# First stage of a hybrid attention block: the hand-written order of weight splits, column sums and products

## The chip, the core and the metric

The kernel runs on one core of a Trainium2 chip. The metric is the device time of one execution in microseconds (us). The engines are TensorE (PE in the profile, its weight loads PEld), VectorE (DVE), ScalarE (ACT), GpSimd (POOL) and the queue that issues transfers (SP). Each engine works through its own instructions in the order in which they stand.

## The reference, cut to what matters

Only the part that the first stage computes is shown. `c` is one vector of 2048, `x` is 512 tokens by 2048, `w_ada` is 2048 by 12288 and `w_in` 2048 by 5664, all f32.

```python
mod = silu(c) @ w_ada + b_ada
sh1, sc1, g1, sh2, sc2, g2 = split(mod, 6)
u = rmsnorm(x) * norm_attn * (1 + sc1) + sh1
z = u @ w_in            # columns: q, k, v of 8 heads, then q, k, v of the sparse branches
...                     # attention, output projection, second norm, SwiGLU, final norm
```

## The kernel before

The first stage makes `sh1` and `sc1` and, as they come out, the first columns of `z`. It is one loop over `step`, written out by hand and kept in that order on all engines (`tc.manual_schedule()`). Eight steps make a block; block `j` handles 256 columns of each of `sc1` and `sh1`, that is two chunks of `u`. There are eight blocks, 64 slots, and `SLOTS + 8` steps or as many as the products need.

Each step does the following, in this order.

- SP issues the tile `ad` of slot `step`: two transfers of 256 KB from `w_ada`, into one of `ADW` = 8 buffers. At the third step of a block (`r == 2`) it also issues the parts of `w_in` for this block (`w_pairs`): `s1` (128x768) and one part of 128x1024 in blocks 0 to 3, two of these in blocks 4 to 7 (blocks from `HJ` = 4 on). The 128x1024 parts share three buffers.
- The slot before it is summed: `acc += ad * silu(c)`. A tile has two halves. Both are added on DVE (L493 for the first of a block, L495 for the rest), or one of them on PE where `on_pe(n)` holds. A **column sum** on PE (L502) is one matmul of 128x512 into the bank `rows`; it stands two steps after its tile. After the last column sum of a block ACT copies `rows` out (L506, the tile `row`).
- `LAGS[0]` = 2 steps after the last slot of a block, sixteen matmuls with one column each (L514, eight records for `row` and eight for `acc`) fold both sums into `sums`. One step later DVE adds the bias (`mod`, L522), makes `a_vec` and `mt` (L386), and ACT makes `uh` (L388). One more step later DVE makes `ul` (L392). `uh` and `ul` are the high and low parts of two chunks of `u`.
- Then products are taken from the list `todo`. A **product** (`unit`) is three matmuls of 128x512 (L255, L256, L257: uh with wh, ul with wh, uh with wl). Products into `S0` stand in the tables as `pss` and `pso`, those of `s1` into `S1` as `psmm`.
- At the end of the step, at `r` = 0, 2, 4, a weight part of the block before is split: ACT casts it to `wh` (L239), DVE subtracts to `wl` (L240).

The bank tag `mm` has four banks. `S1` holds three, so `rows` and `sums` take turns in the fourth: the first column sum of a block waits until `mod` has read `sums`. After the loop, `st.close()` frees the stage's tiles, SP loads the tile `ca` and the next weights, ACT and DVE take `S1` out of its banks, and the next projection (`z_qn`) starts with products into `psmm`.

Of the kernel before, what the change touches and what calls it, by code (L numbers as in the profile page):

```python
# [20 lines left out]
ND = D // P  # L21
# [4 lines left out]
EPS = 1e-6  # L26
ADW = 8
LAG = 2
LAGS = 2, 3, 4
R_C, R_D, R_F, R_V = 1.0, 1.0, 1.0, 0.6  # L30
SCALE = HD ** -0.5
NCMP = 31
# [33 lines left out]
def _pi_parts():  # L66
    out, rest = [], TWO_PI
    for _ in range(3):
        e = 2.0 ** (np.floor(np.log2(rest)) - 7)
        v = np.floor(rest / e) * e  # L70
        out.append(float(v))
        rest -= v
    out.append(float(np.float32(rest)))
    return out
# [3 lines left out]
def hymba_block(ctx: ExitStack, tc: tile.TileContext, x, c, positions, w_ada, b_ada, norm_attn,  # L78
# [21 lines left out]
    def uid(s):  # L100
        n_uid[0] += 1
        return f"{s}_{n_uid[0]}"
# [6 lines left out]
    def bank(tag, shape=(P, T)):  # L109
        return ps.tile(list(shape), F32, tag=tag, name=uid("ps" + tag), bufs=SETS[tag])  # L110
# [258 lines left out]
    def scale_vec(which, i0, n):  # L369
        s0 = (1 if which == 0 else 4) * ND + i0  # L370
        nv = n_attn if which == 0 else n_ffn
        nc.vector.scalar_tensor_tensor(a_vec[:, which, i0:i0 + n], mod[:, s0:s0 + n], 1.0,
                                       nv[:, i0:i0 + n], op0=OP.add, op1=OP.mult)
# [9 lines left out]
    def modulate_a(which, i, src, rb, pl):  # L383
        sh = mod[:, (0 if which == 0 else 3) * ND + i:(0 if which == 0 else 3) * ND + i + 1]
        t = pl.tile([P, T], F32, tag="mt", name=uid("mt"), bufs=2)
        nc.vector.scalar_tensor_tensor(t, src, a_vec[:, which, i:i + 1], rb, op0=OP.mult, op1=OP.mult)  # L386
        h, l = act_tile("u", i)
        nc.scalar.activation(h, t, AF.Identity, bias=sh)  # L388
        return h, l, t, sh
# [7 lines left out]
    def tables():  # L397
        nonlocal cosT, sinT
        cosT = wts.tile([P, T], F32, tag="cos", name="cosT")
        sinT = wts.tile([P, T], F32, tag="sin", name="sinT")  # L400
        ang = posi.bitcast(F32)
        nc.scalar.copy(ang, posi)
        nc.vector.tensor_scalar(ang, ang, cs[:, K_FRQ:K_FRQ + 1], None, op0=OP.mult)
        yield
        for dst, turn in ((sinT, 0.0), (cosT, 0.25)):
            kk = mid.tile([P, T], F32, tag="wx", name=uid("kk"))
            nc.vector.tensor_scalar(kk, ang, 1.0 / TWO_PI, turn, op0=OP.mult, op1=OP.add)
            yield
            nc.vector.tensor_scalar(kk, kk, MAGIC, None, op0=OP.add)
            yield  # L410
            nc.vector.tensor_scalar(kk, kk, MAGIC, None, op0=OP.subtract)
            yield
            cur = ang
            for pc in _pi_parts():
                nc.vector.scalar_tensor_tensor(dst, kk, -pc, cur, op0=OP.mult, op1=OP.add)
                cur = dst
                yield
            if turn:
                nc.vector.tensor_scalar(dst, dst, TWO_PI / 4, None, op0=OP.add)
                yield  # L420
            nc.vector.tensor_scalar(dst, dst, PI_C, -PI_C, op0=OP.min, op1=OP.max)
            yield
        for dst in (sinT, cosT):
            nc.scalar.activation(dst, dst, AF.Sin)

    S0 = [bank(t) for t in BANKS_B]
    S1 = [bank("mm") for _ in range(3)]
# [5 lines left out]
    NJ = ND // 2  # L433
    HJ = NJ // 2

    def w_pairs(j):
        s1 = fetch_w(p_s1, j, src=early, width=3 * P, bufs=2)
        if j < HJ:
            return [fetch_w(p_qn, j), s1]
        i = 2 * (j - HJ)  # L440
        return [fetch_w(p_cmp, i), s1, fetch_w(p_cmp, i + 1)]

    def unit(w, k, i, n, m, outs):
        return lambda: bank_pieces(("ws", m * P, P, outs[m]))[0](w[0], w[1], k, u[i], i == 0, i == n - 1)

    def units(w, pr, outs, n):
        return [unit(w, k, 2 * pr + k, n, m, outs) for k in range(2) for m in range(len(outs))]
# [14 lines left out]
    def due(step, what):  # L462
        for n in range(7, SLOTS, 8):
            if step == n + LAGS[what]:
                return n

    def on_pe(n):
        j, r = divmod(n, 8)
        return r < 7 if j == 0 else 4 <= r < 7

    tiles, accs, rows, sums, halves, fetched, todo = {}, {}, {}, {}, {}, {}, []
    extra_work = tables()
    step = 0
    while step < SLOTS + 8 or todo:
        j, r = divmod(step, 8)
        if j < NJ:
            tiles[step] = early.tile([P, 2, T], F32, tag="adw", name=uid("ad"), bufs=ADW)
            for i, sec in ((0, 1), (1, 0)):
                c0 = sec * D + j * 256
                nc.sync.dma_start(tiles[step][:, :, i * 256:(i + 1) * 256],  # L480
                                  w_ada[:, c0:c0 + 256].rearrange("(q p) n -> p q n", p=P)[:, 2 * r:2 * r + 2, :])
        if r == 2 and j < NJ:
            fetched[j] = w_pairs(j)
        n = step - 1
        if 0 <= n < SLOTS:
            jj, q0 = n // 8, 2 * (n % 8)
            if q0 == 0:
                accs[jj] = early.tile([P, T], F32, tag="acc", name=uid("acc"), bufs=2)
            acc = accs[jj]
            for q in range(1 if on_pe(n) else 2):  # L490
                sc1 = sl[:, q0 + q:q0 + q + 1]
                if q0 + q == 0:
                    nc.vector.tensor_scalar(acc, tiles[n][:, q, :], sc1, None, op0=OP.mult)  # L493
                else:
                    nc.vector.scalar_tensor_tensor(acc, tiles[n][:, q, :], sc1, acc, op0=OP.mult, op1=OP.add)  # L495
        n = step - 2
        if 0 <= n < SLOTS and on_pe(n):
            jj, q = n // 8, 2 * (n % 8) + 1
            first = n == 0 or not on_pe(n - 1)
            if first:  # L500
                rows[jj] = bank("mm")
            nc.tensor.matmul(rows[jj], sl[:, q:q + 1].to_broadcast([P, P]), tiles[n][:, 1, :],  # L502
                             start=first, stop=not on_pe(n + 1))
            if not on_pe(n + 1):
                row = early.tile([1, T], F32, tag="row", name=uid("row"), bufs=2)
                nc.scalar.copy(row, rows[jj][0:1, :])  # L506
                rows[jj] = row
        n = due(step, 0)
        if n is not None:
            jj = n // 8  # L510
            sums[jj] = bank("mm")
            for av, one in ((rows.pop(jj), one_col[0:1, :]), (accs.pop(jj), one_col)):
                for i in range(4):
                    nc.tensor.matmul(sums[jj][:, i:i + 1], av[:, i * P:(i + 1) * P], one,  # L514
                                     start=one is not one_col and i == 0, stop=one is one_col,
                                     skip_group_check=True)
        n = due(step, 1)
        if n is not None:
            jj = n // 8
            for k2, sec in ((0, 1), (1, 0)):  # L520
                m0 = sec * ND + 2 * jj
                nc.vector.tensor_tensor(mod[:, m0:m0 + 2], sums[jj][:, 2 * k2:2 * k2 + 2], b_mod[:, m0:m0 + 2],  # L522
                                        op=OP.add)
            scale_vec(0, jj * 2, 2)
            pend = [modulate_a(0, i, xT[:, i, :], rstd1, early) for i in (2 * jj, 2 * jj + 1)]
        n = due(step, 2)
        if n is not None:
            u.extend([modulate_b(*h) for h in pend])
            jj = n // 8
            if jj < HJ:  # L530
                todo += units(halves[jj][0], jj, S0, ND // 2)
            todo += units(halves[jj][1], jj, S1, ND)
            if jj == HJ - 1:
                todo.append(keep_half)
        for _ in range(2 if step < 8 * HJ + LAGS[2] else 3):
            if todo:
                todo.pop(0)()
        if 0 < j <= NJ and r % 2 == 0 and r // 2 < len(fetched[j - 1]):
            i = r // 2
            w = fetched[j - 1][i]()  # L540
            halves.setdefault(j - 1, []).append(w)
            pr = 2 * (j - 1 - HJ) + i // 2
            if j > HJ and i != 1:
                todo += units(w, pr, S0, ND)
        next(extra_work, None)
        step += 1
    for i in range(ND):
# [672 lines left out]
    for s in range(S):  # L1220
# [19 lines left out]
        n, i = divmod(s - A0, 4)  # L1240
# [108 lines left out]
```

## Time and profile before

| | |
|---|---|
| time before, median of 3 runs | 2492.42 us (2486.96 to 2494.61) |
| time of the profiled execution | 2492.57 us |
| its span, first to last instruction | 2490.0 us |
| mean granted PE clock over the span | 0.973 |
| PE busy | 2364.9 us, 95% of the span |
| DVE busy | 1576.4 us, 63% |
| ACT busy | 1015.3 us, 41% |

The first stage is the first tenth of the span: the page's row of the granted clock has tenths 8 or 9 there, and the row of PE starts with 6, 6, 8. The median and the profiled execution agree within 0.2 us.

### The profile page before, as it was taken

How to read it: one execution, taken by the hardware profiler on the slowest of the kernel's cores; microseconds unless marked ns; L12 is line 12 of the kernel's file. 1: busy time of each engine (PE TensorE's matmuls, PEld its weight loads, DVE VectorE, ACT ScalarE, POOL GpSimd, SP SyncE). 2: the span in 40 equal slices, each digit the busy share in tenths (PEclk: the TensorE clock that was granted, in tenths of full speed). 3: DMA queues.
4: the chain of work that ended last, by engine and by line, in shares of the span. 5: the costliest groups of instructions: out<-in, count | busy, mean ns of one | idle time of the engine just before them, and what ended most of it. 6: DMA issues, size and time to landing. Idle time of an engine off the chain costs nothing.

```text
span 2490.0 us, 38488 instructions
## 1 busy us (share of the span) xinstructions
PE 2364.9 (95%) x14715; PEld 2108.0 (85%) x14715; DVE 1576.4 (63%) x2712; ACT 1015.3 (41%) x1531; POOL 345.4 (14%) x370
## 2 busy tenths in 40 slices
PE   6689899999999999989999999999999899999998
PEld 4467787788887877779999999999999888888887
DVE  6655787877756556587777777777776633333333
ACT  2112544443433332256555555555555522222233
POOL 0001200200010212152121222121221100000010
PEclk8899999999999999989999999999999999999999
DMA  9655454444546257838989899889878653333322
GB/s 321 215 182 171 149 171 138 127 130 140 161 142 193 85 170 253 260 86 211 230 214 226 216 227 225 220 221 228 220 186 205 179 176 132 127 118 122 103 93 102
DMA packets 322713, 440.31 MB, mean 177 GB/s; under 512 B 26224, under 2 KB 217552, under 8 KB 322528
## 3 DMA queue, kind: packets, MB, share of 16 engines
q1 hardware_dynamic: 289104, 348.21, 43.4%
q0 software_dynamic: 31120, 85.45, 18.4%
q10 hardware_dynamic: 2304, 4.20, 0.4%
q8 instruction: 115, 1.88, 0.3%
q14 instruction: 70, 0.57, 0.1%
HBM read 340.18 MB, written 28.38 MB: 148 GB/s over the span
## 4 chain that ended last, share of the span: by engine, by line
PE 53%; DVE 1%; issue 0%; ACT 0%; DVEq 0%; ACTq 0%
PE py L1106 11%; PE py L1109 11%; PE py L1108 11%; PE psmm L257 3%; PE psmm L255 3%; PE psmm L256 3%; PE pss L255 2%; PE pss L256 2%; PE pss L257 2%; PE pso L257 1%; PE pso L256 1%; PE pso L255 1%; PE pso L1006 0%; PE psmm L1316 0%; DVE ul L1089 0%
## 5 line engine op out<-in xcount | busy, mean ns | idle before, releaser
L240 DVE TENSOR_TENSOR wl<-wr,wh 128x1024 fp32r<-128x1024 f32 (+2 forms) x210 | 236.5, 1126 | 413.8 <-ACT wh L239 412.2
L1109 PE MATMUL py<-uh,ls 128*128 128x256 f32 x1408 | 398.4, 283 | 3.8 <-DVE ls L1055 3.8
L1106 PE MATMUL py<-uh,hs 128*128 128x256 f32 x1408 | 399.4, 284 | 1.0 <-DVE ev L1123 0.5
L1108 PE MATMUL py<-ul,hs 128*128 128x256 f32 x1408 | 397.5, 282 | 2.5 <-DVE ul L1089 2.5
L239 ACT CAST wh<-wr 128x1024 fp32r<-128x1024 f32 (+2 forms) x210 | 198.7, 948 | 490.8 <-PE psmm L256 203.3
L1049 ACT CAST hs<-sum 128x1024 fp32r<-128x1024 f32 x176 | 184.7, 1050 | 380.0 <-PE py L1108 254.1
L1055 DVE TENSOR_TENSOR ls<-sum,hs 128x1024 fp32r<-128x1024 f32 x176 | 215.3, 1224 | 194.9 <-ACT hs L1049 194.9
L1108 PE MATMUL py<-ul,hx 128*128 128x256 f32 x1056 | 299.4, 284 | 3.9 <-DVE ul L1089 3.9
L1106 PE MATMUL py<-uh,hx 128*128 128x256 f32 x1056 | 299.0, 283 | 1.7 <-ACT uh L1088 1.4
L1109 PE MATMUL py<-uh,lx 128*128 128x256 f32 x1056 | 299.1, 283 | 0.0
L1109 PEld LDWEIGHTS py<-uh,ls 128*128 128x128 f32 x1408 | 266.8, 189 | 4.8 <-DVE ls L1055 4.8
L1108 PEld LDWEIGHTS py<-ul,hs 128*128 128x128 f32 x1408 | 266.7, 189 | 3.8 <-DVE ul L1089 3.8
L1106 PEld LDWEIGHTS py<-uh,hs 128*128 128x128 f32 x1408 | 267.5, 190 | 2.7 <-DVE ev L1123 1.3
L1045 POOL DMA_DIRECT2D lx<-raw x176 | 156.2, 888 | 593.0 <-ACT lx L1044 437.7
L1108 PEld LDWEIGHTS py<-ul,hx 128*128 128x128 f32 x1056 | 200.3, 190 | 5.1 <-DVE ul L1089 5.0
L1106 PEld LDWEIGHTS py<-uh,hx 128*128 128x128 f32 x1056 | 200.6, 190 | 2.2 <-ACT uh L1088 1.7
L1109 PEld LDWEIGHTS py<-uh,lx 128*128 128x128 f32 x1056 | 200.4, 190 | 0.0
L358 DVE SCALAR_TENSOR_TENSOR acc<-ad,sl,acc 128x512 f32<-128x512 f32 x180 | 139.5, 775 | 49.1 <-DMA ad<-in_w_ada_dram 47.5
L1044 ACT ACTIVATE lx<-raw 128x768 fp32r<-128x768 f32 x176 | 147.9, 840 | 2.5 <-DMA raw<-in_w_gate_dram 2.5
L1040 ACT CAST hx<-raw 128x768 fp32r<-128x768 f32 x176 | 144.3, 820 | 5.8 <-DMA raw<-in_w_gate_dram 5.8
L255 PE MATMUL psmm<-fh,wh 128*128 128x512 f32 x352 | 137.0, 389 | 0.0
L257 PE MATMUL psmm<-fh,wl 128*128 128x512 f32 x352 | 136.9, 389 | 0.0
(441 smaller groups left out, 5308.5 us busy)
## 6 DMA issues: line engine op xcount, KB each, us to landing
lx<-raw POOLq DMA_DIRECT2D x176, 384.0 KB, 5.2
ad<-in_w_ada_dram SPq DMA_DIRECT2D x128, 512.0 KB, 4.2
raw<-in_w_up_dram SPq DMA_DIRECT2D x176, 256.0 KB, 4.1
raw<-in_w_gate_dram SPq DMA_DIRECT2D x176, 256.0 KB, 4.5
wr<-in_w_down_dram SPq DMA_DIRECT2D x88, 512.0 KB, 3.6
ad<-in_w_ada_dram SPq DMA_DIRECT2D x128, 256.0 KB, 5.6
wr<-in_w_in_dram SPq DMA_DIRECT2D x104, 256.0 KB, 3.2
wr<-in_w_in_dram SPq DMA_DIRECT2D x24, 512.0 KB, 4.9
```

Source lines behind the costliest of these rows:

```text
L239: nc.scalar.copy(wh[:, :, s], v)
L240: lo.tensor_tensor(wl[:, :, s], v, split_ap(wh)[:, :, s], op=OP.subtract)
L255: nc.tensor.matmul(dst, wh[:, k, w], ah, start=first, stop=False)
L256: nc.tensor.matmul(dst, wh[:, k, w], al, start=False, stop=False)
L257: nc.tensor.matmul(dst, wl[:, k, w], ah, start=False, stop=last)
L1044: nc.scalar.activation(lx[s], raw[s][:, 1:4, :], AF.Copy, scale=-1.0)
L1045: nc.gpsimd.dma_start(split_ap(lx[s]), raw[s][:, 1:4, :], accum_op=OP.add)
L1049: nc.scalar.copy(hs[s], sums[s])
L1055: nc.vector.tensor_tensor(ls[s], sums[s], split_ap(hs[s]), op=OP.subtract)
L1106: nc.tensor.matmul(o, wh[:, wi, js], vh[:, vi, :], start=k == 0 and j == 0, stop=False, skip_group_check=True)
L1108: nc.tensor.matmul(o, wh[:, wi, js], vl[:, vi, :], start=False, stop=False, skip_group_check=True)
L1109: nc.tensor.matmul(o, wl[:, wi, js], vh[:, vi, :], start=False, stop=k == KG - 1, skip_group_check=True)
```

## The change

The order of the loop's work is changed; the work itself is nearly the same. Weight parts are split at the head of a step instead of its end, at `r` = 0, 1, 3. Column sums sit at slots 2 to 5 of blocks 1 to 4 (four instead of three) and at slots 2 and 3 of blocks 5 to 7 (two instead of three); block 0 keeps its seven. That is 29 column sums instead of 28. Up to step 37 one product is taken at each step, two while more than `KEEP` = 12 are left, instead of two; from step 38 on three. Products of `s1` in blocks 4 to 7 are put into the list two steps later.

```diff
-LAGS = 2, 3, 4
+LAGS = 2, 3, 4, 6
+KEEP = 12
...
     def on_pe(n):
         j, r = divmod(n, 8)
-        return r < 7 if j == 0 else 4 <= r < 7
+        return r < 7 if j == 0 else 2 <= r < (6 if j <= HJ else 4)
...
+    AT = {0: 0, 1: 1, 3: 2}
...
         if r == 2 and j < NJ:
             fetched[j] = w_pairs(j)
+        i = AT.get(r, 3)
+        if 0 < j <= NJ and i < len(fetched[j - 1]):
+            w = fetched[j - 1][i]()
+            halves.setdefault(j - 1, []).append(w)
+            pr = 2 * (j - 1 - HJ) + i // 2
+            if j > HJ and i != 1:
+                todo += units(w, pr, S0, ND)
...
             if jj < HJ:
-                todo += units(halves[jj][0], jj, S0, ND // 2)
-            todo += units(halves[jj][1], jj, S1, ND)
+                todo += units(halves[jj][0], jj, S0, ND // 2) + units(halves[jj][1], jj, S1, ND)
             if jj == HJ - 1:
                 todo.append(keep_half)
-        for _ in range(2 if step < 8 * HJ + LAGS[2] else 3):
+        n = due(step, 3)
+        if n is not None and n // 8 >= HJ:
+            todo += units(halves[n // 8][1], n // 8, S1, ND)
+        for _ in range(3 if step >= 8 * HJ + LAGS[3] else 1 + (len(todo) > KEEP)):
             if todo:
                 todo.pop(0)()
-        if 0 < j <= NJ and r % 2 == 0 and r // 2 < len(fetched[j - 1]):
-            i = r // 2
-            w = fetched[j - 1][i]()
-            halves.setdefault(j - 1, []).append(w)
-            pr = 2 * (j - 1 - HJ) + i // 2
-            if j > HJ and i != 1:
-                todo += units(w, pr, S0, ND)
```

Three places show how rows move. In the changed kernel the lines named above stand a little lower: L255 to L257 become L256 to L258, L502 becomes L511, L506 L515, L514 L523, L388 L389, L239 L240. SP and POOL have the same instructions in the same order in both, and behind the first products of `z_qn` so have the other engines.

The first place is PE where the `u` of block 1 comes in (`uh_101`, `ul_102` before, `uh_103`, `ul_104` with the change; `pss_45` is the first bank of `S0`, `psmm_49` to `psmm_51` are `S1`). Before:

```order
L514 MATMUL psmm_96_487<-cs_71,row_91_468 128x1 x4
L514 MATMUL psmm_96_487<-cs_71,acc_70_358 128x1 x4
L255 MATMUL psmm_50_283<-uh_80_392,wh_82_395 128x512
L256 MATMUL psmm_50_283<-ul_81_393,wh_82_395 128x512
L257 MATMUL psmm_50_283<-uh_80_392,wl_83_396 128x512
L255 MATMUL psmm_51_284<-uh_80_392,wh_82_395 128x512
L256 MATMUL psmm_51_284<-ul_81_393,wh_82_395 128x512
L257 MATMUL psmm_51_284<-uh_80_392,wl_83_396 128x512
L255 MATMUL pss_45_278<-uh_101_518,wh_92_476 128x512
```

The same place with the change, from the first column sum of block 2 (`psmm_110`) on:

```order
L511 MATMUL psmm_110_533<-ad_99_489,sl_112 128x512
L256 MATMUL psmm_49_282<-uh_82_396,wh_70_358 128x512
L257 MATMUL psmm_49_282<-ul_83_397,wh_70_358 128x512
L258 MATMUL psmm_49_282<-uh_82_396,wl_71_359 128x512
L256 MATMUL psmm_50_283<-uh_82_396,wh_70_358 128x512
L257 MATMUL psmm_50_283<-ul_83_397,wh_70_358 128x512
L258 MATMUL psmm_50_283<-uh_82_396,wl_71_359 128x512
L511 MATMUL psmm_110_533<-ad_108_517,sl_112 128x512
L256 MATMUL psmm_51_284<-uh_82_396,wh_70_358 128x512
L257 MATMUL psmm_51_284<-ul_83_397,wh_70_358 128x512
L258 MATMUL psmm_51_284<-uh_82_396,wl_71_359 128x512
L256 MATMUL pss_45_278<-uh_103_504,wh_92_456 128x512
```

Before, two old products stand between the folding and the first product with new `u`; with the change seven old products and two column sums do (four of the products stand ahead of this piece).

The second place is ACT from the `row` of block 1 on, in the next block. Before:

```order
L506 COPY row_91_468<-psmm_88_441 1x512
L239 CAST wh_92_476<-wr_75_378 128x1024
L388 ACTIVATE uh_101_518<-mt_100_516,mod_276 128x512
L388 ACTIVATE uh_104_523<-mt_103_521,mod_276 128x512
L239 CAST wh_106_526<-wr_74_375 128x768
```

With the change:

```order
L515 COPY row_90_447<-psmm_86_417 1x512
L240 CAST wh_92_456<-wr_77_382 128x1024
L240 CAST wh_95_469<-wr_76_379 128x768
L389 ACTIVATE uh_103_504<-mt_102_502,mod_276 128x512
L389 ACTIVATE uh_106_509<-mt_105_507,mod_276 128x512
```

The casts of both weight parts still stand behind the copy of `row`; the second cast has moved ahead of `uh`.

The third place is PE at the end of the loop. Before, the last product goes into `S0` (`pso_168`) and `z_qn` (`psmm_274`, `psmm_275`) follows:

```order
L255 MATMUL pso_168_865<-uh_256_1354,wh_260_1390 128x512
L256 MATMUL pso_168_865<-ul_257_1355,wh_260_1390 128x512
L257 MATMUL pso_168_865<-uh_256_1354,wl_261_1391 128x512
L255 MATMUL psmm_274_1487<-uh_179_911,wh_279_1493 128x512
L256 MATMUL psmm_274_1487<-ul_180_912,wh_279_1493 128x512
L255 MATMUL psmm_275_1488<-uh_179_911,wh_279_1493 128x512
```

With the change:

```order
L256 MATMUL psmm_51_284<-uh_258_1352,wh_251_1320 128x512
L257 MATMUL psmm_51_284<-ul_259_1353,wh_251_1320 128x512
L258 MATMUL psmm_51_284<-uh_258_1352,wl_252_1321 128x512
L256 MATMUL psmm_274_1487<-uh_177_885,wh_279_1493 128x512
L257 MATMUL psmm_274_1487<-ul_178_886,wh_279_1493 128x512
L258 MATMUL psmm_274_1487<-uh_177_885,wl_280_1494 128x512
```

Before, the eight products of the last 128x1024 part stood behind the last product into `S1`; now a product into `S1` is the last of the loop, and in `z_qn` the first matmul with `wl` is the third instead of the sixth.

## Rows read from the trace of the kernel before

**Rows 1.** The page's head.
```profile
span 2490.0 us, 38488 instructions
```
**Rows 2.** Busy time by window: PE, PEld, DVE, ACT, POOL, then granted clock, DMA share, GB/s.
```profile
88.00:112.00 24.00, 16.87 (x64) 12.20 (x64) 14.64 (x24) 3.63 (x5) 0.00 (x0) 0.86 0.74 237
...
189.00:210.00 21.00, 19.22 (x81) 14.30 (x79) 12.98 (x20) 4.59 (x6) 0.00 (x0) 0.95 0.94 337
```
**Rows 3.** Waits from 20 to 215 us: total us, times, longest.
```profile
ACT row L506 <- PE psmm L502: 110.2, 8, 17.6
DVE wl L240 <- ACT wh L239: 61.1, 15, 8.6
...
PE pss L256 <- DVE ul L392: 16.0, 4, 4.0
...
PE pss L255 <- ACT uh L388: 13.6, 4, 4.9
```
**Rows 4.** PE in order of time: start us, us, instruction, idle before and its releaser.
```profile
105.09 1.02 PE L502 MATMUL psmm<-ad,sl 128*128 128x512 f32 x2
...
106.18 0.40 PE L256 MATMUL psmm<-ul,wh 128*128 128x512 f32 x1
106.42 0.39 PE L257 MATMUL psmm<-uh,wl 128*128 128x512 f32 x1
...
107.44 1.05 PE L514 MATMUL psmm<-cs,row 1*128 1x1 f32 x8
...
109.33 0.48 PE L255 MATMUL psmm<-uh,wh 128*128 128x512 f32 x1
...
113.92 0.50 PE L255 MATMUL pss<-uh,wh 128*128 128x512 f32 x1 [2.94 <-ACT uh L388]
118.41 0.79 PE L256 MATMUL pss<-ul,wh 128*128 128x512 f32 x1 [4.00 <-DVE ul L392]
```
**Rows 5.** ACT in order of time, the same block.
```profile
106.51 0.58 ACT L506 COPY row<-psmm 1x512 f32<-1x512 f32 x1 [15.06 <-PE psmm L502]
107.00 1.04 ACT L239 CAST wh<-wr 128x1024 fp32r<-128x1024 f32 x1
```
**Rows 6.** DVE in order of time, the same block.
```profile
108.07 1.23 DVE L240 TENSOR_TENSOR wl<-wr,wh 128x1024 fp32r<-128x1024 f32 x1 [7.46 <-ACT wh L239]
109.21 0.48 DVE L493 TENSOR_SCALAR acc<-ad,sl 128x512 f32<-128x512 f32 x1
109.73 2.33 DVE L495 SCALAR_TENSOR_TENSOR acc<-ad,sl,acc 128x512 f32<-128x512 f32 x3
111.97 0.22 DVE L522 TENSOR_TENSOR mod<-psmm,vec 128x2 f32<-128x2 f32 x2
...
112.36 1.42 DVE L386 SCALAR_TENSOR_TENSOR mt<-xT,a_vec,rstd 128x512 f32<-128x512 f32 x2
115.28 0.96 DVE L240 TENSOR_TENSOR wl<-wr,wh 128x768 fp32r<-128x768 f32 x1 [1.51 <-ACT wh L239]
...
117.61 1.41 DVE L392 SCALAR_TENSOR_TENSOR ul<-mt,mod,uh 128x512 fp32r<-128x512 f32 x2
```
**Rows 7.** SP's transfers in order of time, block 4.
```profile
119.00 17.94 SPq L223 DMA_DIRECT2D wr<-in_w_in_dram  x4
```
**Rows 8.** PE in order of time, behind a folding without idle time (L514, 184.55 to 186.44).
```profile
187.70 0.63 PE L257 MATMUL pss<-uh,wl 128*128 128x512 f32 x1
188.13 0.63 PE L255 MATMUL pss<-uh,wh 128*128 128x512 f32 x1
...
191.10 0.39 PE L256 MATMUL pss<-ul,wh 128*128 128x512 f32 x1
```
**Rows 9.** DVE in order of time: the first `mod` of the stage.
```profile
41.19 0.22 DVE L522 TENSOR_TENSOR mod<-psmm,vec 128x2 f32<-128x2 f32 x2
```
**Rows 10.** PE in order of time, end of the loop and start of `z_qn`.
```profile
221.41 0.39 PE L255 MATMUL pss<-uh,wh 128*128 128x512 f32 x1
...
230.18 0.50 PE L255 MATMUL psmm<-uh,wh 128*128 128x512 f32 x1 [3.14 <-ACT wh L239]
```

## The prediction, made before the changed kernel ran

> **What bounds the kernel now.** I read the busy table by windows first, since the change touches only the first stage, then the waits of that stage, then one block engine by engine. The reader is to see that no engine is full there. In the third block, 24 us long, PE is busy for 16.9 us, DVE for 14.6, ACT for 3.6, and the transfers run at 237 GB/s, where a later window has 337 [rows 2]. The time goes to a loop through four engines. PE comes to the last column sum of a block at 105.09 with products before it in its row [rows 4]. Only then can ACT copy `row` out (106.51), and the cast behind that copy ends near 108.05 [rows 5]. DVE, idle for 7.46 us, splits the weight part at 108.07 and needs until 111.97 to reach `mod` [rows 6]. PE meanwhile does two products, runs out, and stands idle 2.94 us for `uh` and 4.00 us for `ul` [rows 4]. In sum ACT waits 110.2 us for column sums and DVE 61.1 us for the casts behind them; PE waits 16.0 and 13.6 us for the new `u` in the four blocks that end in `pss` [rows 3].
>
> Three prices follow. A product is three matmuls; at full clock one starts 0.24 us after the other (106.18 to 106.42), so I take 0.70 us. A column sum starts 1.09 us before the matmul that stands two places behind it (105.09 to 106.18), where one step would be 0.23: it costs 0.86. A folding (L514) takes 1.9 us (107.44 to 109.33) [rows 4]. At the low clock a matmul starts 0.43 us behind the last (187.70 to 188.13). Such a stretch lasts some 3.4 us (to 191.10) and loses 3.4 x (1 - 0.23/0.43) = 1.6 us [rows 8].
>
> **The change part by part.** It adds one column sum on PE, 0.86 us, and takes one sum from DVE, 0.75 us [rows 6]; both lie in the sum below. Nothing else is added or removed, and SP's order is the same; so what counts is who waits for whom. I follow the changed order from `mod` to `mod` with the prices of before.
>
> Block 1. In block 0 the split of 128x1024 now stands ahead of the last two sums on DVE and the 128x768 split ahead of `mod`, so the first `mod` comes later: 41.19 [rows 9] becomes about 42.1. The cast that DVE had to wait 1.51 us for [rows 6] is done by then, and between `mod` and `ul` stand only `mt` (1.4), one sum and a table step: PE starts at 45.7. Until its last column sum PE has five products and four column sums, 6.9 us, and 1.6 us lost to the low clock it starts with: 54.2. Then `row` and cast 1.56 [rows 5], the split 1.14, two sums 1.5, the split of 128x768 0.9, the first sum 0.5, three sums 2.24 [rows 6], and 0.7 of table work left between them: `mod` of block 1 at 62.7.
>
> Blocks 2 and 3. The loop is still there, because the casts still stand behind `row`, but it is shorter: four column sums with six products between them (7.6), `row` and cast 1.56, split 1.14, two sums 1.5, split 0.9, first sum 0.5, three sums 2.24: 15.5 us. The first column sum waits for `mod` (they share a bank), which closes the loop. At the folding PE still stands about 2 us, so I charge most of a stretch at the low clock, 1.4: 16.9 us a block in place of about 24 (the window of [rows 2] runs from one `mod` to the next). `mod` of block 3 comes at 62.7 + 33.8 = 96.5. DVE has less than 15.5 us of work in such a block. Eight tiles and the weight parts are 5.1 MB a block, which at 337 GB/s [rows 2] is 15.1 us, inside 16.9, with up to eight tiles already there.
>
> From block 4 on the list holds more products than PE can do while the loop goes round, so PE sets the time. In block 4 it starts the column sums 2.5 us behind `mod`, spends 8.3 us on four of them and seven products, then does six products (4.2) and the folding (1.9): 113.4. What is left for PE then is counted from the changed order: 95 products (66.5), six column sums (5.2), three foldings (5.7), together 77.4. I add 1.1 us for the low clock behind each of the last four foldings (between nothing and the 1.6 of [rows 8]) and 1.5 for the copies of `part` that the new bank group has to wait for; the bounds of that wait are nothing and the 2.9 us that `uh` cost PE [rows 4]. The loop ends at 113.4 + 77.4 + 4.4 + 1.5 = 196.7.
>
> The clock is where a rule of the Trainium skill and the rows part. In [rows 8] PE had no idle time, only the one-column matmuls of a folding, and its matmuls went from 0.23 to 0.43 us. The page TensorE: Matmul & The Clock Gate (section What's actually happening) says that the low clock is the default, activity lifts it, and a spell of idleness brings it back. By that rule the four stretches without idle time would not come, and the sum would be 4.4 us shorter; the trace does not agree with it here.
>
> The end of the loop costs something back. Before, the last product into `S1` ends at 221.41 and `z_qn` starts 8.8 us later, at 230.18; but 5.6 us of that are filled with the products of the last 128x1024 part, and PE idles only 3.14 [rows 10]. What runs in those 8.8 us (freeing the tiles, loading and splitting the next weights) hangs on the last product into `S1`, which is now the last of all. So PE idles the whole 8.8 us. Its order in `z_qn` has three matmuls fewer ahead of the first `wl`: 0.7 more. `z_qn` starts at 196.7 + 9.5 = 206.2 in place of 230.2: 24.0 us earlier. Behind it all orders are the same, and I take the gain through whole. The profiled execution's own time, 2492.57 beside its span of 2490.0 [rows 1] and practically the median (2492.42), becomes 2468.6, rounded to 2469.
>
> **The rivals.** (a) The clock holds through the foldings, and the 2 us at them shrink: the 4.4 us and two to three times 1.4 come off, with a little less at the copies 8 to 12 in all, 2459. For it: after the change PE has products on both sides of a folding. Against it: [rows 8]. The rule named above is a reason of its own for this case.
>
> (b) The loop shortens less: if DVE, ACT and PE don't fall into step in blocks 1 to 3 and each takes some 4 us more, and the end costs what I say, 12 us of the 24 are left: 2481. For it: each handover in the four-engine loop was priced without delay, and in [rows 6] a 1.51 us wait stood where the order alone shows none.
>
> (c) Slower: the third part of `w_in` in blocks 4 to 7. Its buffer comes free only when an older part is split, and SP, which stands still for it (17.94 us with its four transfers, [rows 7]), issues no tiles meanwhile. Now PE's first column sums are at the third and fourth slot of a block, the very tiles behind that part, and all products stand behind them. In my account the split comes some 15 us of PE work ahead of those sums, so that the tiles land in time. If they came 8 us late in each of blocks 5 to 7, the gain would be gone; above 10.5 us in each, the kernel is slower by 0.3% or more, about 2500. Against it: at the head of a step the split comes earlier than before, and SP stands still for less.
>
> (d) The change does not do what it says: if PE is dry again at each `uh`, because the old products are done before `mod`, only the earlier casts (1.5 us in each of seven blocks) are won, and the end takes 6.3 back: 2488, no change that can be measured.
>
> **How the numbers follow.** A measurement of this kernel tells about 0.3% (7.5 us) from no change. My forecast, a gain of 16 to 31 us (2462 to 2477), gets 0.58; (a), more than that, 0.14; (b), 8 to 16 us, 0.14; (d) and what else ends within 7.5 us, 0.08; (c) 0.06. Faster by over 0.3%: 0.58 + 0.14 + 0.14 = 0.86; same 0.08; slower 0.06. The range runs from 2454, where (a) takes all its terms and the waits go too, to 2484, the worst of (b); about two in ten lie outside. The predicted time is the forecast's, 2469.
>
> **What would show it.** In the changed profile: `mod` (L531 there) eight times, the first near 42, then near 63, 80, 97, 115, 135, 157 and 178; PE's waits for `uh` and `ul` gone but for block 0; DVE's waits for `wh` in blocks 1 to 3 at 2 to 3 us each instead of 7; transfers well over 237 GB/s in the third block; in the blocks from the fifth on PE busy nearly throughout; an idle time of 8 to 9 us on PE ahead of `z_qn`, near 197 to 206. PE idle for tiles in blocks 5 to 7 would make (c) right; `uh` waits of 3 us in each block (d); no matmul pair 0.43 us apart behind the foldings of blocks 4 to 7 (a). I would be wrong altogether if the last stages gave the time back, which nothing in the rows suggests.

## The result, and the profile of the changed kernel

The changed kernel takes 2464.91 us (median of 4 runs, 2460.09 to 2470.78) where the kernel before, run beside it, takes 2491.72 (2486.96 to 2494.61): a ratio of 0.9895, 95% interval 0.9866 to 0.9924. It is 26.8 us faster; 24.0 were forecast. The profiled execution has a span of 2469.0 us and took 2470.78.

The eight `mod` rows on DVE are the pulse of the first stage. Columns: start us, us, instruction, idle time before and who ended it.

```profile
42.18 0.22 DVE L531 TENSOR_TENSOR mod<-psmm,vec 128x2 f32<-128x2 f32 x2
63.34 0.22 DVE L531 TENSOR_TENSOR mod<-psmm,vec 128x2 f32<-128x2 f32 x2
80.30 0.22 DVE L531 TENSOR_TENSOR mod<-psmm,vec 128x2 f32<-128x2 f32 x2
97.82 0.22 DVE L531 TENSOR_TENSOR mod<-psmm,vec 128x2 f32<-128x2 f32 x2
116.03 0.22 DVE L531 TENSOR_TENSOR mod<-psmm,vec 128x2 f32<-128x2 f32 x2
136.14 0.23 DVE L531 TENSOR_TENSOR mod<-psmm,vec 128x2 f32<-128x2 f32 x2 [0.20 <-PE psmm L523]
156.50 0.23 DVE L531 TENSOR_TENSOR mod<-psmm,vec 128x2 f32<-128x2 f32 x2 [1.62 <-PE psmm L523]
178.40 0.23 DVE L531 TENSOR_TENSOR mod<-psmm,vec 128x2 f32<-128x2 f32 x2 [5.14 <-PE psmm L523]
```

The forecast was 42, 63, 80, 97, 115, 135, 157 and 178. Blocks 2 and 3 take 17.0 and 17.5 us instead of about 24. From the sixth row on `mod` itself waits for PE's folding (L523): PE, no longer the loop, sets the time. The busy time by window (columns as in [rows 2]) says the same. PE is busy for 22.66 of 24 us in the window where it had 16.87 [rows 2], and for practically all of the last four windows:

```profile
88.00:112.00 24.00, 22.66 (x91) 16.72 (x89) 15.65 (x24) 5.90 (x8) 0.00 (x0) 0.93 0.80 255
```

```profile
80.00:98.00 18.00, 16.66 (x64) 12.19 (x64) 13.97 (x24) 3.64 (x5) 0.00 (x0) 0.88 0.97 309
...
116.00:136.00 20.00, 19.62 (x84) 15.07 (x82) 17.53 (x27) 5.65 (x8) 0.00 (x0) 0.93 0.90 283
136.00:156.00 20.00, 20.00 (x91) 15.70 (x91) 16.32 (x24) 4.69 (x6) 0.00 (x0) 1.00 0.94 303
156.00:178.00 22.00, 22.00 (x95) 17.29 (x95) 13.67 (x20) 4.58 (x6) 0.00 (x0) 0.92 0.72 260
178.00:195.00 17.00, 16.98 (x76) 13.65 (x75) 4.32 (x8) 2.32 (x3) 0.00 (x0) 1.00 0.00 0
```

The waits from 20 to 215 us that answer to [rows 3] (total us, times, longest): ACT's wait for the column sums is halved, so is DVE's for casts, and of PE's 29.6 us for new `u` nothing is left but one wait each for `uh` and `ul` in block 0 (4.1 and 0.8 us). Part of that comes back elsewhere: at the foldings of blocks 0 to 3 PE waits 8.0 us for DVE's last sums.

```profile
ACT row L515 <- PE psmm L511: 55.5, 8, 10.3
DVE wl L241 <- ACT wh L240: 30.9, 12, 6.9
...
PE psmm L523 <- DVE acc L504: 8.0, 4, 2.6
...
PE pss L256 <- ACT uh L389: 4.1, 1, 4.1
```

Last, the end of the loop on PE, which answers to [rows 10]. The last product starts at 194.59, PE idles 8.51 us, and `z_qn` starts at 203.49: 26.7 us earlier than before. DVE's part of the first weight comes 1.18 us later still.

```profile
194.59 0.39 PE L258 MATMUL psmm<-uh,wl 128*128 128x512 f32 x1
203.49 0.79 PE L256 MATMUL psmm<-uh,wh 128*128 128x512 f32 x1 [8.51 <-ACT wh L240]
204.08 0.63 PE L257 MATMUL psmm<-ul,wh 128*128 128x512 f32 x1
205.88 0.80 PE L258 MATMUL psmm<-uh,wl 128*128 128x512 f32 x1 [1.18 <-DVE wl L241]
```

### The profile page after: what moved, and what is told of

Its sections match the earlier page's. It is cut to its first block, busy times and chain, and to the rows that moved or that the text cites. A ratio compares the mean times of both kernels' runs of the same rounds, so it can differ in the third digit from the quotient of the medians.

```text
span 2469.0 us, 38501 instructions
## 1 busy us (share of the span) xinstructions
PE 2363.4 (96%) x14717; PEld 2108.9 (85%) x14717; DVE 1578.9 (64%) x2711; ACT 1015.6 (41%) x1531; POOL 342.6 (14%) x370
## 4 chain that ended last, share of the span: by engine, by line
PE 54%; DVE 1%; issue 0%; DMA 0%; ACT 0%; DVEq 0%; ACTq 0%
PE py L1110 11%; PE py L1113 11%; PE py L1112 11%; PE psmm L256 3%; PE psmm L258 3%; PE psmm L257 3%; PE pss L256 2%; PE pss L257 2%; PE pss L258 2%; PE pso L256 1%; PE pso L258 1%; PE pso L257 1%; PE pso L1010 0%; DMA out_dram<-ot 0%; DVE ul L1093 0%
## 5 line engine op out<-in xcount | busy, mean ns | idle before, releaser
L240 ACT CAST wh<-wr 128x1024 fp32r<-128x1024 f32 (+2 forms) x210 | 198.5, 949 | 502.6 <-PE psmm L257 214.4
L1059 DVE TENSOR_TENSOR ls<-sum,hs 128x1024 fp32r<-128x1024 f32 x176 | 215.3, 1223 | 195.0 <-ACT hs L1053 195.0
L256 PE MATMUL psmm<-uh,wh 128*128 128x512 f32 x306 | 130.6, 427 | 8.9 <-ACT wh L240 8.9
L256 PE MATMUL psmm<-fh,wh 128*128 128x512 f32 x352 | 137.0, 389 | 0.0
```

Of the source, the lines that this page charges most:

```text
L240: nc.scalar.copy(wh[:, :, s], v)
L256: nc.tensor.matmul(dst, wh[:, k, w], ah, start=first, stop=False)
L1059: nc.vector.tensor_tensor(ls[s], sums[s], split_ap(hs[s]), op=OP.subtract)
```

## The experiments

Two theories stood against each other. **L**: the four-engine loop limits the blocks, and everything that shortens it helps. **H**: what helps is only that PE has products in hand while the loop goes round. The change has three parts: **head** (weight parts split at the head of steps 0, 1 and 3 instead of the end of 0, 2 and 4), **sums** (the column sums from the third slot of a block instead of the fifth) and **pace** (one product a step while twelve or fewer are in the list, three late in the stage, and the products into `S1` queued later). The runs cover all eight combinations. I read two numbers from each trace: where `z_qn` starts, and where the loop ends, which is that start less PE's idle time ahead of it. Both come from one execution of each kernel; the loop ends of the changed kernel, e12 and e5, which are alike up to the last block, differ by 1.6 us.

| parts in the kernel | run | median us | ratio to before (95%) | loop ends | idle | `z_qn` |
|---|---|---|---|---|---|---|
| none | before | 2491.72 | 1 | 227.0 | 3.14 | 230.18 |
| head | e1 | 2483.86 | 0.9957 (0.9941 to 0.9974) | 208.3 | 8.51 | 216.76 |
| pace | e2 | 2476.24 | 0.9927 (0.9912 to 0.9943) | 202.3 | 8.51 | 210.82 |
| sums | e3 | 2479.24 | 0.9941 (0.9925 to 0.9956) | 210.8 | 3.13 | 213.94 |
| head, pace | e4 | 2467.38 | 0.9890 (0.9875 to 0.9904) | 189.2 | 8.51 | 197.69 |
| head, sums | e7 | 2484.79 | 0.9959 (0.9944 to 0.9974) | 213.2 | 8.51 | 221.66 |
| pace, sums | e9 | 2461.09 | 0.9878 (0.9863 to 0.9893) | 188.8 | 8.51 | 197.33 |
| all three | changed | 2464.91 | 0.9895 (0.9866 to 0.9924) | 195.0 | 8.51 | 203.49 |
| all three | e12, again | 2468.85 | 0.9906 (0.9891 to 0.9921) | 194.0 | 8.51 | 202.48 |

The kernel before ran again beside each group of experiments: 2495.11 us beside e1 to e4, 2495.28 beside e5 to e8, 2493.16 beside e9 to e12.

**One part alone: e1, e2, e3.** e1 is the kernel before with the splits moved from the end of a step to its head, e2 with the pacing (the line shown, and the products into `S1` queued as in the change), e3 with the one line of `on_pe`:

```
e1   +        i = AT.get(r, 3)
     ...
     -        if 0 < j <= NJ and r % 2 == 0 and r // 2 < len(fetched[j - 1]):
     ...
e2   +        for _ in range(3 if step >= 8 * HJ + LAGS[3] else 1 + (len(todo) > KEEP)):
     ...
e3   +        return r < 7 if j == 0 else 2 <= r < (6 if j <= HJ else 4)
```

> The kernel before with one part of the change: weight parts split at the head of a step (r = 0, 1, 3); column sums and the pace of the products as before. Theory L (up to block 4 the stage is a loop through PE, ACT and DVE, in which the casts stand behind the copy of row): with sums at slots 4 to 6 the first cast now stands ahead of that copy, so DVE's waits for casts of 6 to 9 us go, and each of blocks 1 to 4 gets 3 to 5 us shorter; the end loses its 6 us, since the products into S1 become the last here too. z_qn starts at 212 to 220 (230.2 before, 203.5 with the whole change), the time is 10 to 18 us below before. Theory H (what counts is only that PE has old products in hand while new u are made): PE runs dry as before, so the start of z_qn stays within 4 us of 230 or comes later by the lost end.

> The kernel before with one part of the change: products taken one a step (two while more than twelve are left), three from step 38 on, those of s1 put into the list later; column sums and split places as before. Theory H: PE has products in hand behind each folding, its waits for uh and ul go, and most of the gain is here: z_qn at 205 to 212, 18 to 25 us below before. Theory L: the casts still stand behind row, and row behind the last column sum, which sits later in the block than in the changed kernel; fewer products stand ahead of it, so each block gets some 2 to 3 us shorter: z_qn at 215 to 223, 7 to 15 us below before.

> The kernel before with one part of the change: column sums at slots 2 to 5 of blocks 1 to 4, 2 and 3 of the later ones; split places and pace as before. Theory L: the last column sum has about four products fewer ahead of it, so row, casts and mod come up to 2.8 us earlier in each block, in blocks 5 to 7 more: z_qn at 208 to 220, 10 to 20 us below before. Theory H: PE is dry for uh and ul as before; z_qn within 4 us of 230.

Each part gains alone: 11, 19 and 16 us. e1 and e3 lie where L put them, and H's "nothing" is refuted; e2 is where H put it, below L's band, though PE still waits 9.8 us in sum for `ul`, a wait that H expected to go. So both are at work, and the pace is the largest single part (in time it and the sums are not told apart). Added up, the loop would end 18.8 + 24.7 + 16.2 = 59.7 us earlier; with all three it ends 32.1 earlier. They overlap, which the pairs show better.

**Two parts: e4, e7, e9.** Each is the changed kernel with one part as before (in e7 the queueing of `S1` too, in e9 the split at the step's end):

```
e4   -        return r < 7 if j == 0 else 2 <= r < (6 if j <= HJ else 4)
     +        return r < 7 if j == 0 else 4 <= r < 7
     ...
e7   -        for _ in range(3 if step >= 8 * HJ + LAGS[3] else 1 + (len(todo) > KEEP)):
     +        for _ in range(2 if step < 8 * HJ + LAGS[2] else 3):
     ...
e9   -        i = AT.get(r, 3)
     ...
     +        if 0 < j <= NJ and r % 2 == 0 and r // 2 < len(fetched[j - 1]):
```

> The whole change, but column sums at slots 4 to 6 as before. Theory L: the cast of the 128x1024 part stands ahead of row on ACT then, so the 3 to 4.4 us for which DVE waits for casts in blocks 1 to 4 of the changed kernel go, and blocks 2 to 4 take 14.5 to 16 us instead of 17 to 18; blocks 5 to 7 have one sum more each on PE (0.86): z_qn at 197 to 204, time equal to the whole change or up to 6 us below. Theory H, and the thought that early sums are a part of the gain: equal or slower, z_qn at 204 to 210.

> The whole change without its pacing: splits at the head and column sums early, but two products a step, and products into S1 queued as before. e1 and e3 moved z_qn by 13.4 and 16.3 us to 216.8 and 213.9; the whole change has 203.5. Theory L (the loop is shortened by the casts and by the sums, each on its own): blocks 2 and 3 take 17-20 us each, and z_qn starts at 205-212. Theory H (the products in hand make the gain, the others only come into their own with them): PE runs out of products at each folding again, waits for uh and ul over 10 us in sum, and z_qn starts at 212-218. In both PE idles about 3.1 us ahead of z_qn, since the products into S0 stand last as in the kernel before.

> The whole change without its third part: pacing and early column sums, but the weight parts split at the end of a step as before. Pacing alone has z_qn at 210.8, the whole change at 203.5. Theory L (the casts behind row close the loop, and the split at the head takes them forward): DVE waits longer for its casts, and z_qn comes at 206-212. Rival H (with the products paced, PE has work while the loop goes round, and where the split stands doesn't matter): z_qn within 2.5 us of the whole change, 201-206.

e4 lies where L put it. e9 lies where neither put it: at 197.33 its `z_qn` comes 6.2 us ahead of the whole change, so where the split stands does matter, but with the sign opposite to L's. e7 misses both: its `z_qn` comes at 221.66, and the idle time of 8.51 us was not foreseen either (it stands wherever head or pace is in, since products into `S1` then come last). PE's waits for `uh`, 13.0 us in sum, are those that H asked for.

What the eight combinations show is something else. The pace is worth 18 to 25 us of loop whatever it is added to (227.0 to 202.3 alone, 208.3 to 189.2 with head, 210.8 to 188.8 with sums, 213.2 to 195.0 with both); in time that is 14 to 19 us. But head and sums spoil each other: beside the pace either one ends the loop near 189, both together at 195. Without the pace both together (213.2) are worse than either alone (208.3, 210.8). In time e7 is not told apart from either one alone, nor e4 from the whole change. In e9, with the split where it was, the kernel is faster than the whole change on the same chip (2459.84 to 2463.39 against e12's 2466.69 to 2468.97).

The fifth `mod`, behind which PE sets the time, shows where they do so. With the whole change it comes at 116.03. The pace alone (e2), the pace with head (e4) and the pace with sums (e9) have it at:

```profile
115.73 0.22 DVE L523 TENSOR_TENSOR mod<-psmm,vec 128x2 f32<-128x2 f32 x2
```

```profile
104.33 0.22 DVE L531 TENSOR_TENSOR mod<-psmm,vec 128x2 f32<-128x2 f32 x2
```

```profile
110.30 0.23 DVE L523 TENSOR_TENSOR mod<-psmm,vec 128x2 f32<-128x2 f32 x2 [0.49 <-PE psmm L515]
```

So up to there head gains 11.4 us beside the pace, sums 5.4, and both together nothing. From the fifth `mod` to the end of the loop e4 needs 84.9 us, e9 and the whole change 78.5 and 79.0: there the new slots do pay. They save three column sums, 2.6 us at the 0.86 of the prediction, and the wait for the copies of `part`, 2.50 us in e4, is 0.38 in the changed kernel; the rest is not explained. The old slots up to block 4 with the new ones behind them were not tried.

The reason for the loss up to the fifth `mod` stands in one block of each. ACT, then DVE, of the changed kernel:

```profile
90.04 0.58 ACT L515 COPY row<-psmm 1x512 f32<-1x512 f32 x1 [7.20 <-PE psmm L511]
90.53 1.77 ACT L240 CAST wh<-wr 128x1024 fp32r<-128x1024 f32 x2
```

```profile
91.60 1.23 DVE L241 TENSOR_TENSOR wl<-wr,wh 128x1024 fp32r<-128x1024 f32 x1 [3.71 <-ACT wh L240]
92.75 1.53 DVE L504 SCALAR_TENSOR_TENSOR acc<-ad,sl,acc 128x512 f32<-128x512 f32 x2
94.19 0.95 DVE L241 TENSOR_TENSOR wl<-wr,wh 128x768 fp32r<-128x768 f32 x1
95.06 0.48 DVE L502 TENSOR_SCALAR acc<-ad,sl 128x512 f32<-128x512 f32 x1
95.58 2.33 DVE L504 SCALAR_TENSOR_TENSOR acc<-ad,sl,acc 128x512 f32<-128x512 f32 x3
97.82 0.22 DVE L531 TENSOR_TENSOR mod<-psmm,vec 128x2 f32<-128x2 f32 x2
```

ACT and DVE of e9, the same place of block 3:

```profile
87.78 0.58 ACT L507 COPY row<-psmm 1x512 f32<-1x512 f32 x1 [6.60 <-PE psmm L503]
88.26 1.04 ACT L240 CAST wh<-wr 128x1024 fp32r<-128x1024 f32 x1
```

```profile
84.07 5.47 DVE L496 SCALAR_TENSOR_TENSOR acc<-ad,sl,acc 128x512 f32<-128x512 f32 x7
89.46 1.22 DVE L241 TENSOR_TENSOR wl<-wr,wh 128x1024 fp32r<-128x1024 f32 x1
90.59 0.48 DVE L494 TENSOR_SCALAR acc<-ad,sl 128x512 f32<-128x512 f32 x1
91.11 2.33 DVE L496 SCALAR_TENSOR_TENSOR acc<-ad,sl,acc 128x512 f32<-128x512 f32 x3
93.35 0.22 DVE L523 TENSOR_TENSOR mod<-psmm,vec 128x2 f32<-128x2 f32 x2
```

From `row` to `mod` the changed kernel needs 7.8 us, e9 5.6. With early column sums the copy of `row` stands ahead of both casts on ACT. A split at the head of a step then stands ahead of the block's last two sums on DVE, which stops 3.71 us with work behind it, and does those sums and the 128x768 split inside the loop. At the end of the step DVE has done its seven sums while ACT casts, and waits for nothing at this place. With the old slots of e4 the copy of `row` comes behind the cast of the 128x1024 part, and its early split waits for nothing in blocks 1 to 4.

**The end of the loop: e5.** It lets the last six products into `S1` go ahead of the last eight into `S0`.

```
+            if jj == NJ - 1:
+                todo[-8:-8] = units(halves[jj][1], jj, S1, ND)
...
-        if n is not None and n // 8 >= HJ:
+        if n is not None and HJ <= n // 8 < NJ - 1:
```

> The whole change, but in the last block the six products into S1 stand ahead of the last eight products into S0 instead of behind them. In the changed kernel PE idles 8.51 us ahead of z_qn (start 203.49). My account (what runs in that time hangs on the last product into S1): the eight products, 5.6 us, fill most of it, the idle time falls to 2.5-3.5 us, z_qn starts at 197.5-199.5, and the kernel is 4-6 us faster than the changed one. Rival (what runs there hangs on something else that ends late, the last split or the last product of all): the idle time stays above 7 us, z_qn starts at 202-204.5, the time is within 2 us of the changed kernel's.

2462.97 us, ratio 0.9877 (0.9863 to 0.9891). The row of PE:

```profile
196.50 0.80 PE L256 MATMUL psmm<-uh,wh 128*128 128x512 f32 x1 [3.13 <-ACT wh L240]
```

The idle time falls by 5.38 us, close to the 5.6 us that the prediction had counted as lost at the end. The rest of the 7.0 us at `z_qn`, which puts it a little ahead of its band, is a loop that ended 1.6 us earlier. Against the kernel before this is 32.3 us, where the changed kernel has 26.8 and 24.3 in its two series: the medians lie as expected, but the gain in time of 4 to 6 us is not settled, since the intervals overlap or touch. The idle time of 3.13 us came again in e8 and e10, which have the same edit (3.13 and 3.14).

**The casts ahead of `row`: e6.** The other way out of what e9 shows: keep the early sums, and split two steps earlier.

```
+        if j < HJ and r in (5, 6):
+            halves.setdefault(j, []).append(fetched[j][r - 5]())
...
-        if 0 < j <= NJ and i < len(fetched[j - 1]):
+        if HJ < j <= NJ and i < len(fetched[j - 1]):
```

> The whole change, but both w_in parts of blocks 0 to 3 are split in the sixth and seventh step of their own block, so that their casts stand ahead of the row copy on ACT and no longer behind it. In the changed kernel DVE waits 4.10, 3.14, 3.71 and 4.39 us for these casts in blocks 1 to 4. Theory L (the loop of blocks 1 to 4 closes through the casts): these waits fall below 1 us, the mod of the fifth block comes at 102-111 instead of 116.0, and z_qn starts 3-8 us earlier, at 195.5-200.5. Theory H (only the products in hand matter; PE has the same work in any order): the waits fall, but mod moves to another wait (PE's column sums), the fifth mod stays within 3 us of 116.0 and z_qn at 201-205. A third way: the parts are not in place yet in the sixth step, DVE waits for transfers instead, and the fifth mod comes after 118.

2460.87 us, ratio 0.9866 (0.9851 to 0.9880); the fifth `mod` at 107.70, `z_qn` at 195.15, a little ahead of L's band. The waits for casts ahead of the second to fourth `mod` are down to 1.54 and 1.87 us in all, though not below 1 us as L had them; one of 5.25 us, at 101.48, stays, since it is for block 4's own part, which the edit leaves in place. L is borne out here, and with it the place where the loop closes: the casts.

**Together: e8 and e10.** e8 is e4 with the edit of e5; e10 adds the edit of e6.

> The changed kernel with the old slots of the column sums (as e4) and with the products into S1 of the last block ahead of the last eight into S0 (as e5). e4 had z_qn at 197.7 with an idle time of 8.51 us ahead of it. If both edits add up: idle time 2.5-3.5, z_qn at 191-194, and 6-12 us faster than the changed kernel, the time 2453-2460 where the kernel before has 2493. If they don't (the time behind z_qn gives it back, as some us of the whole change's gain went between z_qn and the end): z_qn early all the same, but the time within 4 us of the changed kernel's.

> e8 (old slots of the column sums, last products reordered) with the splits of blocks 0 to 3 taken into their own block as in e6. e8 has z_qn at 192.9; e6 took 8.3 us from the changed kernel there. With the old slots the row copy stands behind the casts anyway. Theory L: so there is hardly anything left to win, DVE's waits for casts stay small, z_qn 190.5-193.5, the time within 3 us of e8's. Rival: early splits are worth the same here as in e6, z_qn 184-189. Other side: the parts are not in place in the sixth step, since the blocks are only 14.5 us long now; DVE waits for transfers, z_qn after 194.

e8: 2455.62 us (2453.01 to 2459.55), ratio 0.9847 (0.9832 to 0.9862), `z_qn` at 192.86 with an idle time of 3.13. It beats both kernels, by 39.7 us the one before. e10: 2459.02, 0.9870 (0.9853 to 0.9886), `z_qn` at 191.38, in L's band; in time it is not told apart from e8, and nothing more is won. Why not, the windows of e8 tell, from `mod` to `mod` in block 3 and 4 and the 15.2 us behind:

```profile
73.70:88.20 14.50, 13.82 (x60) 10.15 (x60) 14.15 (x23) 3.63 (x5) 0.00 (x0) 0.96 1.08 352
88.20:104.80 16.60, 16.60 (x70) 12.47 (x69) 14.23 (x23) 3.64 (x5) 0.00 (x0) 0.91 1.07 342
104.80:120.00 15.20, 13.94 (x54) 10.45 (x52) 11.40 (x19) 4.34 (x6) 0.00 (x0) 0.91 0.80 250
```

In the first DVE is busy for 14.15 of 14.5 us and the transfers run at 352 GB/s, in the second PE is busy throughout: up to the fifth `mod` (104.84 in e8, 103.36 in e10) hardly anything is left to shorten. In the third no engine is full, but e10's edit does not reach it, and from the fifth `mod` to the end of the loop both need 84.9 us. (e9 with the edit of e5 was not tried.)

**The low clock behind a folding: e11 and e12.** e11 folds `row` one step earlier than `acc`, with products between; e12 is the changed kernel again.

```
+        n = due(step, 4)
+        if n is not None:
+            sums[n // 8] = bank("mm")
+            fold(n // 8, rows.pop(n // 8), one_col[0:1, :])
+            if todo:
+                todo.pop(0)()
...
```

> The whole change with the folding of each block in two halves of eight one-column matmuls: that of row one step earlier, then one to three products, then that of acc. In the changed kernel PE is at the low clock for 3.4-3.8 us behind the foldings that end near 61, 78, 95, 115.6 and 156.3, the last two without any idle time ahead. If the unbroken 1.9 us of one-column matmuls bring the clock down: no matmuls 0.43 us apart behind the foldings of the last four blocks, and z_qn 2-5 us earlier, 198.5-201.5. If it is idle time alone (the low clock at 115.6 and 156.3 has another cause): stretches of the low clock at as many places as before, z_qn within 1.5 us of 203.5, or later by as much as PE now waits for row.

> The changed kernel as it is, beside the others on one chip. Its first runs gave 2464.91 us and z_qn at 203.49; I expect a ratio of 0.987-0.992 to the kernel before, z_qn at 203-204, and the low clock behind the same foldings (115.6 and 156.3, not 136 and 178) if it goes by the order of the work, behind others if it goes by chance.

In the changed kernel's profile PE had no idle time at the foldings of blocks 4 to 7. Behind two of them the clock fell; the folding here ends near 114.1:

```profile
113.20 1.05 PE L523 MATMUL psmm<-cs,acc 128*128 128x1 f32 x8
...
115.12 0.40 PE L257 MATMUL psmm<-ul,wh 128*128 128x512 f32 x1
115.36 0.44 PE L258 MATMUL psmm<-uh,wl 128*128 128x512 f32 x1
115.59 0.63 PE L256 MATMUL psmm<-uh,wh 128*128 128x512 f32 x1
116.02 0.63 PE L257 MATMUL psmm<-ul,wh 128*128 128x512 f32 x1
```

Matmuls follow 0.43 us apart from 115.59, and again from 156.73; behind the foldings of blocks 5 and 7 they don't. The granted clock of the windows above says the same: 0.93 and 0.92 in the two that hold these stretches, 1.00 in the other two. In e12, the same program, it is block 5 alone:

```profile
134.03 1.05 PE L523 MATMUL psmm<-cs,acc 128*128 128x1 f32 x8
134.94 0.47 PE L256 MATMUL psmm<-uh,wh 128*128 128x512 f32 x1
...
136.32 0.63 PE L258 MATMUL psmm<-uh,wl 128*128 128x512 f32 x1
136.75 0.63 PE L256 MATMUL psmm<-uh,wh 128*128 128x512 f32 x1
```

The time is as expected, `z_qn` (202.48) half a us ahead of its band, and the second case holds: the order of the work does not decide alone where the clock falls. In e11 it falls behind none of the four, and the loop ends near 191.3, 2.6 to 3.6 us earlier than in the two profiles of the whole change. That is what the first theory asked for. The traces of e4, e5, e6, e8, e9 and e10 have the same foldings in one piece, with PE busy ahead of them: with the two above, such a stretch stands behind 12 of 32, at least one in each of the eight profiles. Beside that e11's none of four leans to the first theory, but one profile can be luck, and the time, 2463.82 us, 0.9889 (0.9871 to 0.9908), is not told apart from the whole change. What brings the clock down there stays open.

## Why the prediction was right, step by step

**Block 1** was to bring `mod` at 62.7 from a first one at 42.1: 63.34 and 42.18.

**Blocks 2 and 3** were priced at 16.9 us: 16.96 and 17.52. The loop closes as described, with `row`, cast, split, two sums, split and four sums in a chain; e6 and e9, which open this chain at the cast, take the blocks to 15.2 to 15.6 and 15.5. PE stands 2.01 and 1.34 us at the foldings ("about 2 us"). DVE's waits for the casts of blocks 1 to 3 were put too low, at 2 to 3 us: they are 4.10, 3.14 and 3.71. And the charge for the low clock is no constant: in e12, the same program, block 3 took 19.13 us, with matmuls 0.43 us apart from 76.16 to 80.86.

**From block 4 on** PE was to set the time, with the folding of block 4 done at 113.4 and the loop at an end at 196.7. The folding ends at 114.1 and the loop at 195.0. Two terms of the sum behind 113.4 were too large. The 4.4 us of low clock were two stretches of 3.4 and 3.7 us, which by the working of the prediction lose 1.6 and 1.7, 3.3 in sum. The wait for the copies of `part`, put at 1.5 us, was 0.38 us in this profile, but 0.81 and 0.85 us in that of e12:

```profile
123.42 0.50 PE L256 MATMUL pss<-uh,wh 128*128 128x512 f32 x1 [0.38 <-DVE part L455]
```

```profile
119.04 0.50 PE L256 MATMUL pss<-uh,wh 128*128 128x512 f32 x1 [0.81 <-ACT part L457]
...
122.41 0.50 PE L256 MATMUL pss<-uh,wh 128*128 128x512 f32 x1 [0.85 <-DVE part L455]
```

So the wait is real, and its size was right for one of two executions. In e12 one stretch of low clock, 1.4 us by the same working, stands beside it. The two terms come to 3.7 and 3.1 us where 5.9 were put. Since both vary between executions, a part of the closeness is luck.

**The rule of the clock.** The section What's actually happening of the Trainium skill's page TensorE: Matmul & The Clock Gate (activity lifts the clock, a spell of idleness brings it back) would have no low stretch without idle time. The traces show two and one of four such foldings with one: neither the rule nor my four of four.

**The end.** PE idles 8.51 us, where 8.8 were put. The 0.7 us for the order in `z_qn` should not have stood in its start: they fall behind it, where PE idles 1.18 us ahead of the first `wl` (0.99 before). So `z_qn` starts at 203.49, forecast 206.2. Taking the gain through whole held roughly: over e1 to e12 the gain in time is within 5 us of the gain at `z_qn`, from 10.5 us for 8.5 (e7) to 39.7 for 37.3 (e8); the widest gaps are e4 (27.7 for 32.5) and e10 (34.1 for 38.8).

**The rivals.** (a) fell by half: low stretches came, but fewer. (b): blocks 1, 2 and 3 cost 0.6, 0.1 and 0.6 us more than priced, not 4. (c): SP stood 9.74, 7.90 and 5.87 us with the four transfers for the weight parts of blocks 5 to 7, where before it was 17.94 [rows 7], 14.68 and 13.34, and PE was never late for its tiles in these blocks. (d): PE's waits for `uh` were gone but for block 0.

**What the prediction did not see** is that a part of the change works against the whole. It counted the split at the head of a step as a gain, since its cast would be done by then (true of the 128x768 part). It had the 128x1024 split, two sums and the second split in its own chain, and never asked what the chain would be with the split left where it was: 5.6 us from `row` to `mod` in place of 7.8. The sum for the whole was right all the same, because the cost stood in it unnamed. It also treated the new slots as one thing, where they cost in blocks 1 to 4, beside the split at the head, and pay in blocks 5 to 7.

## What to carry to other kernels

In a loop through several engines, list for each engine what stands between the instruction that is released and the one that releases the next: work that could be done during the wait belongs ahead of the waiting instruction, and an instruction moved "earlier" may only carry its wait, and what is queued behind it, into the loop. Work kept in hand for the engine that would run dry added its gain to every other variant; two edits that mend the same wait did not add up. Price a change with one part left out as well, since the whole may be worse than its best part, and price it stage by stage, since one edit may pay in one stage and cost in another.

## What was not expected of the hardware

The same program had the low clock behind the foldings of blocks 4 and 6 in one profile and of block 5 in another, each without idle time ahead, for 3.0 to 3.7 us at 0.43 us a matmul instead of 0.23. Of nine profiles with products paced and PE busy ahead of these foldings, the eight with the folding in one piece had at least one such stretch each, the one with it in two halves none; what brings it on is not shown. Where one execution has its stretches of low clock is no property of the program.
